# A two-layer hybrid decoder trunk on one core: the second block's sliding attention weights are turned by VectorE and DRAM, and the delta values' trip by DRAM follows the small inverses

## The chip, the cores and the metric

The kernel runs on one core of one Trainium2 chip. The metric is device time in microseconds (us) of one execution. A core has TensorE for matmuls (PE in the profile, with its weight loads as PEld), VectorE (DVE), ScalarE (ACT), GpSimd (POOL) and SyncE (SP), each with its own queue of instructions; DMAs are issued here by SP and POOL. Transfers of weights are issued by SP, those by DRAM that this text speaks of by POOL.

## The reference

Two decoder layers on 256 tokens of width 1024. Each is a SwiGLU half step, then three token mixers on the same stream (a gated delta rule, a sliding-window attention with sinks, a cross attention to 256 memory rows), a gated merge with an output projection, and another SwiGLU half step, each of the three with a residual and a layer norm. The change touches the sliding attention and the delta rule's values:

```python
def sliding_window_attention(q, k, v, sinks):      # 8 heads in 2 groups of 4, dh 64, window 128
    nb = S_ // W                                   # 2 blocks of 128 queries
    ...
    s = jnp.einsum('bnqhgd,bnkhd->bnhgqk', qb, kb).astype(f32) * (dh ** -0.5)
    ...
    m = jnp.maximum(s.max(-1, keepdims=True), sink)
    p = jnp.exp(s - m)
    p = p / (p.sum(-1, keepdims=True) + jnp.exp(sink - m))
    o = jnp.einsum('bnhgqk,bnkhd->bnqhgd', p.astype(v.dtype), vb)

def gated_delta_rule(q, k, v, g, beta):            # 4 heads, dk = dv = 128, chunks of 64
    ...
    sol = lax.linalg.triangular_solve(t_mat, rhs, left_side=True, lower=True, unit_diagonal=True)
```

A query block sees its own 128 keys and, for the second block, the 128 before them. So the weights p of the first block have one key block and those of the second have two.

## The kernel before, in words

All 256 tokens stay on the chip. Weights come as a stream of units of 128 x 1024 numbers: SP loads a unit into `raw`, ACT casts it to `whi` and DVE computes the remainder `wlo` (`unit`, line 104; `split`, line 124). Each product is three matmuls (`mm3`, line 139), high by high, high by low, low by high. The pool of `whi` has five buffers and that of `wlo` too (lines 42 and 43), so a unit's cast takes the buffer of the unit five before it and waits until PE has done that unit's matmuls.

`mixers` (line 560) holds the token mixers. Its matmuls are pinned: `keep_in_program_order` puts PE's work in the order in which the code is written. `weave` (line 145) runs a generator of matmul groups and calls small steps behind the group of a given number. ACT, DVE and POOL are ordered by a scheduler when the program is built; `issue_after` adds that an instruction stands behind another on the same engine's queue, and `held` does so for the last recorded instruction of each engine in the dictionary `late`. Within an engine the queue is fixed once the program is built.

The steps around the change, with block `tb` 0 or 1 (the first or second 128 tokens) and `hh` 0 or 1 (the first or second four of the eight heads):

- `w_scores(tb, hh)` (line 803): scores of the sliding attention on PE, mask, maximum, exponential and division on DVE and ACT; the weights stand as queries by keys in `wpr[tb, hh]`. Its reciprocal on DVE is `wpr["end"]`.
- `w_turn(tb, hh)` (line 832): turns them to keys by queries. Four PE transposes a key block (the line is 137, a helper's) into a PSUM bank `at`, then one copy a bank into `wpT[tb]` (line 840, ACT for key block 0, DVE for key block 1). For block 1 that is eight transposes and two copies for each `hh`.
- `w_values(tb)` (line 842): values times weights, two matmuls a key block, into one bank `at`, then a split into `oS` (buffers u6 and u7) by ACT and DVE.
- `inverses` (line 857): 16x16 triangular inverses on POOL in 15 steps, until line 883 writes `Y32`.
- `doubling(c)` (line 913): grows these to 32, 64 and 128, for both token blocks `c`, in steps of matmuls on PE into a bank `sm` and copies of it on ACT or DVE (buffers w0 to w3). `double` (line 970) runs one step of both. Each step's matmuls read what the step before copied.
- `begin_inverse` (line 974): one DVE transpose of `Y32`, which waits for POOL.
- `leave_v`, `back_v`, `land_v` (lines 635 to 650): the delta rule's values go from channels by tokens (`vT`, buffer u8) to tokens by channels (`vin`, u2). DVE turns 32x32 squares into `z`, POOL stores `z` to a DRAM tile `tv` in four DMAs a block (64 KB each, runs of 512 bytes), and loads it back in one DMA a block (256 KB); DVE scales it.
- `gates(n)` (line 1042): sigmoid gates, two halves of four units, twelve matmuls a unit, eight steps. `branch(n, o)` (line 1060): the branch's projection by four units, twelve matmuls a step, four steps; the first two steps read block 0 of `o`, the last two block 1.

The order is written at lines 1078 to 1108: `gates(0)`, `branch(0, oX)`, `gates(1)`, `branch(1, oS)`, `gates(2)`, `branch(2, oT)`. Before the change, `gates(1)` had `leave_v` behind step 3, `w_turn(1, 0)` and `back_v` behind step 5, `w_turn(1, 1)` behind step 6, and `w_values(1)` and `land_v` behind step 7.

## Time and profile before

| | us |
|---|---|
| timed runs, median of 3 | 1265.56 |
| timed runs, lowest to highest | 1264.87 to 1265.59 |
| the profiled execution's own time | 1265.74 |
| its span in the trace | 1263.8 |
| granted TensorE clock, mean | 0.998 |

| engine | busy us | share |
|---|---|---|
| PE | 1252.4 | 99% |
| DVE | 878.2 | 69% |
| ACT | 661.0 | 52% |
| POOL | 235.4 | 19% |

The span is what the trace holds; the execution's time is 1.9 us longer. A row of the timeline gives the start of an instruction (or of several alike, xN), how long it took, engine, line and operation, the tile written and the one read, shapes, and in brackets how long the engine was idle before it and what ended that. Matmuls are pipelined: each row's duration overlaps the next one's start, so the cost of a group on a busy PE is the difference of two starts. The changed steps lie in the two stretches from 325 to 385 us (layer 0) and from 950 to 1010 us (layer 1).

### The profile page before, as it was taken

The numbers are of one execution on the slowest core, as the hardware profiler recorded it, in microseconds if no ns is written. First come the engines' busy times: TensorE is split into PE (matmuls) and PEld (weight loads), VectorE is DVE, ScalarE is ACT, GpSimd is POOL, SyncE is SP. The second block draws the span as 40 slices with busy tenths as digits, with TensorE's granted clock in tenths as the row PEclk, the third lists the DMA queues.
The fourth block names the chain that finished last, engine by engine and source line by source line (L and its number), as shares of the span: only waits on it lengthen the run. The fifth ranks groups of instructions, "written<-read, shape, count | busy, mean of one in ns | idle before, by whom it ended". The sixth has DMA issues, their size and how long they took to land.

```text
span 1263.8 us, 18750 instructions
## 1 busy us (share of the span) xinstructions
PE 1252.4 (99%) x6884; PEld 1067.8 (84%) x6884; DVE 878.2 (69%) x1292; ACT 661.0 (52%) x982; POOL 235.4 (19%) x419
## 2 busy tenths in 40 slices
PE   9999999999999999999999999999999999999997
PEld 6888889999878888888888888899988788888886
DVE  6688567886668776665776665779777587666565
ACT  6456444655664544444354544365647654455441
POOL 1232102002331102221012220020033301122100
PEclk9999999999999999999999999999999999999999
DMA  8988867655554748877668876676564466577872
GB/s 283 317 271 280 262 217 216 224 180 133 170 152 150 242 140 258 243 241 221 221 205 240 260 261 204 213 237 214 163 157 140 130 200 217 184 242 246 243 224 77
DMA packets 80203, 267.76 MB, mean 212 GB/s; under 512 B 12912, under 2 KB 14352, under 8 KB 80112
## 3 DMA queue, kind: packets, MB, share of 16 engines
q1 hardware_dynamic: 66320, 232.40, 56.8%
q0 software_dynamic: 13648, 34.04, 10.5%
q8 instruction: 54, 0.88, 0.3%
q14 instruction: 37, 0.30, 0.1%
q10 hardware_dynamic: 144, 0.13, 0.0%
HBM read 249.58 MB, written 16.94 MB: 211 GB/s over the span
## 4 chain that ended last, share of the span: by engine, by line
PE 98%; DMA 1%; DVE 0%; SPq 0%; issue 0%; ACT 0%; DVEq 0%
PE acc L134 87%; PE at L134 4%; PE sm L134 3%; PE sm L137 1%; PE acc L332 1%; PE acc L333 1%; PE acc L335 1%; PE at L137 1%; DMA raw<-in_wst_dram 1%; DVE h L291 0%; DVE h L296 0%; SPq L115 0%; SPq L78 0%; ACT whi L125 0%; DVE bnst L277 0%
## 5 line engine op out<-in xcount | busy, mean ns | idle before, releaser
L125 DVE TENSOR_TENSOR wlo<-raw,whi 128x1024 fp32r<-128x1024 f32 (+2 forms) x405 | 487.0, 1210 | 258.3 <-ACT whi L125 256.4
L125 ACT CAST whi<-raw 128x1024 fp32r<-128x1024 f32 (+2 forms) x405 | 413.5, 1029 | 391.9 <-PE acc L134 305.3
L134 PE MATMUL acc<-whi,hT 128*128 128x512 f32 (+1 forms) x1824 | 562.9, 386 | 1.1 <-ACT whi L125 1.1
L134 PEld LDWEIGHTS acc<-whi,hT 128*128 128x128 f32 x1824 | 340.5, 188 | 71.6 <-ACT whi L125 2.9
L134 PE MATMUL acc<-wlo,hT 128*128 128x512 f32 (+1 forms) x912 | 350.7, 385 | 0.0
L134 PE MATMUL acc<-whi,u 128*128 128x512 f32 x812 | 259.7, 392 | 0.0
L134 PEld LDWEIGHTS acc<-wlo,hT 128*128 128x128 f32 x912 | 171.7, 188 | 32.8 <-DVE wlo L125 0.7
L134 PEld LDWEIGHTS acc<-whi,u 128*128 128x128 f32 x812 | 152.3, 188 | 32.0 <-DVE u L125 0.5
L134 PE MATMUL acc<-wlo,u 128*128 128x512 f32 x406 | 158.3, 390 | 0.0
L362 POOL DMA_DIRECT2D tr<-t x176 | 96.0, 552 | 315.3 <-DVE t L356 313.1
L134 PE MATMUL acc<-hT,whi 128*128 128x256 f32 x672 | 121.8, 284 | 0.0
L134 PEld LDWEIGHTS acc<-hT,whi 128*128 128x128 f32 x672 | 104.8, 192 | 0.0
L134 PE MATMUL acc<-hT,wlo 128*128 128x256 f32 x336 | 95.2, 283 | 0.0
L134 PEld LDWEIGHTS acc<-wlo,u 128*128 128x128 f32 x406 | 76.3, 188 | 15.4
L134 PEld LDWEIGHTS acc<-hT,wlo 128*128 128x128 f32 x336 | 64.4, 192 | 0.0
L363 POOL DMA_DIRECT2D pt<-tr x44 | 24.6, 558 | 192.1 <-DMA tr<-t 158.7
L353 ACT ACTIVATE t<-acc 128x256 f32<-128x256 f32 x88 | 33.4, 380 | 37.5 <-PE acc L134 37.4
L134 PE MATMUL acc<-u,u 128*128 128x512 f32 x186 | 46.4, 394 | 0.0
L354 DVE TENSOR_TENSOR t<-t,acc 128x256 f32<-128x256 f32 x88 | 36.7, 417 | 8.1 <-ACT t L353 3.9
L134 PEld LDWEIGHTS acc<-u,u 128*128 128x128 f32 x186 | 34.7, 188 | 7.5
L125 DVE TENSOR_TENSOR u<-pt,u 128x512 fp32r<-128x512 f32 x44 | 28.9, 657 | 10.0 <-ACT u L125 9.9
L589 DVE SCALAR_TENSOR_TENSOR t<-acc,cw,t 128x255 f32<-128x255 f32 (+2 forms) x72 | 34.5, 480 | 1.1
(250 smaller groups left out, 1177.1 us busy)
## 6 DMA issues: line engine op xcount, KB each, us to landing
raw<-in_wst_dram SPq DMA_DIRECT2D x409, 512.0 KB, 4.4
tr<-t POOLq DMA_DIRECT2D x176, 64.0 KB, 3.8
pt<-tr POOLq DMA_DIRECT2D x44, 256.0 KB, 5.3
raw<-in_wst_dram SPq DMA_DIRECT2D x16, 324.0 KB, 5.0
gB<-in_lnp_dram SPq DMA_DIRECT2D x6, 512.0 KB, 6.3
bB<-in_lnp_dram SPq DMA_DIRECT2D x6, 512.0 KB, 6.8
tn<-pp POOLq DMA_DIRECT2D x16, 128.0 KB, 3.8
pt<-tn POOLq DMA_DIRECT2D x8, 256.0 KB, 5.8
```

What stands on the lines that cost most here:

```text
L125: return nc.scalar.copy(hi, src).ins, nc.vector.tensor_tensor(lo, src, hi.bitcast(F32), op=ALU.subtract).ins
L134: return pe(nc.tensor.matmul(*a, **k))
L137: return pe(nc.tensor.transpose(*a))
L332: nc.tensor.matmul(ps, hT[0][:, k, ts], hi[:, c], start=k == 0, stop=False)
L333: nc.tensor.matmul(ps, hT[0][:, k, ts], lo[:, c], start=False, stop=False)
L335: nc.tensor.matmul(ps, hT[1][:, k, ts], hi[:, c], start=False, stop=k == KD - 1)
L353: act = nc.scalar.activation(t[:, :, tb, :], g, AF.Silu).ins
L354: ins = nc.vector.tensor_tensor(t[:, :, tb, :], t[:, :, tb, :], u, op=ALU.mult).ins
L362: nc.gpsimd.dma_start(d[:, :, q].rearrange("b c x -> c b x"), z[32 * q:32 * q + 32].rearrange("c (b x) -> c b x", b=4))
L363: back = nc.gpsimd.dma_start(y, d.rearrange("b c q x -> (b c) (q x)")).ins
L589: nc.vector.scalar_tensor_tensor(yc[:, j, d:], b[:, j, :S - d], w[:, t:t + 1], yc[:, j, d:], op0=ALU.mult, op1=ALU.add)
```

## The change

The second block's weights no longer pass PE. `w_turn` keeps the first block only. `w_leave(hh)` is new: two DVE transposes of 32x32 squares a half into `z` (buffers u8 and bB), four POOL stores of 128 KB into a DRAM tile `tw` (runs of 512 bytes), and two POOL loads of 256 KB, one a key block, into `wpT[1]`. The loaded tile has another order of its columns, so `w_values(1)` reads and writes with other access patterns, and its split is in two halves. `w_leave(0)` stands behind step 3 of `gates(1)`, `w_leave(1)` behind step 5, and `w_values(1)` moves from step 7 of `gates(1)` to step 1 of `branch(1, oS)`.

`leave_v` now holds the loads of `back_v` too, and moves from step 3 of `gates(1)` to step 3 of `branch(0, oX)`, ahead of `begin_inverse`: its DVE transposes stand behind `wpr["end"]` and ahead of `begin_inverse`'s, its stores behind `Y32`'s last instruction on POOL, its loads behind its stores.

The diff:

```diff
@@ -633,23 +633,25 @@
             return src[:, :, tb * P:(tb + 1) * P].rearrange("p h (q j) -> p q h j", q=4)
 
         def leave_v():
+            turned_v = []
             for tb in range(2):
                 z = T(p2, [P, 512], "t2", bufs=4)
-                nc.vector.transpose(z, squares(vT, tb))
+                with tc.issue_after(wpr["end"]):
+                    wpr["z"] = nc.vector.transpose(z, squares(vT, tb)).ins
                 d = T(pd, [4, 32, 4, P], "tv")
                 for a in range(4):
-                    nc.gpsimd.dma_start(d[:, :, a].rearrange("t j x -> j t x"), z[32 * a:32 * a + 32].rearrange("j (t x) -> j t x", t=4))
+                    with tc.issue_after(late["inverses"]):
+                        out_ = nc.gpsimd.dma_start(d[:, :, a].rearrange("t j x -> j t x"), z[32 * a:32 * a + 32].rearrange("j (t x) -> j t x", t=4)).ins
                 turned_v.append(d)
-
-        def back_v():
             for tb in range(2):
-                nc.gpsimd.dma_start(vin[:, tb].rearrange("p a h i -> p (a h i)"), turned_v[tb].rearrange("t j a x -> (t j) (a x)"))
+                with tc.issue_after(out_):
+                    late["pool"] = nc.gpsimd.dma_start(vin[:, tb].rearrange("p a h i -> p (a h i)"), turned_v[tb].rearrange("t j a x -> (t j) (a x)")).ins
 
         def land_v():
             for tb in range(2):
                 late["dve"] = nc.vector.tensor_tensor(vin[:, tb], vin[:, tb], kn[:, tb, :].unsqueeze(1).unsqueeze(3).to_broadcast([P, 4, 4, 32]), op=ALU.mult).ins
 
-        turned_v, sums_q = [], []
+        sums_q = []
 
         def leave_q():
             part = T(p2, [P, 4, 8], "oqs")
@@ -827,17 +829,29 @@
                 nc.scalar.activation(pr[:, h, :nk], pr[:, h, :nk], AF.Exp, bias=mxs[:, h // 2, h % 2:h % 2 + 1], accum_out=sums[:, h:h + 1])
             nc.vector.tensor_tensor(sums, sums, flat(sk), op=ALU.add)
             wpr["end"] = nc.vector.reciprocal(sums, sums).ins
-            [nc.scalar.mul(pr[:, h, :nk], pr[:, h, :nk], sums[:, h:h + 1]) for h in range(4)]
-
-        def w_turn(tb, hh):
+            late["act"] = [nc.scalar.mul(pr[:, h, :nk], pr[:, h, :nk], sums[:, h:h + 1]) for h in range(4)][-1].ins
+
+        def w_turn(hh):
             if hh == 0:
-                wpT[tb] = [T(p2, [P, 2, 4, P], "pt") for _ in range(tb + 1)]
-            for kb in range(tb + 1):
-                ps = at().rearrange("p (h k) -> p h k", h=4)
-                for h in range(4):
-                    transpose(ps[:, h, :], wpr[tb, hh][:, h, kb * P:(kb + 1) * P], ident)
-
-                (nc.vector.tensor_copy if kb else nc.scalar.copy)(wpT[tb][kb][:, :, 2 * hh:2 * hh + 2, :].rearrange("p v i q -> p i v q"), ps.rearrange("p (i v) q -> p i v q", v=2))
+                wpT[0] = T(p2, [P, 2, 4, P], "pt")
+            ps = at().rearrange("p (h k) -> p h k", h=4)
+            for h in range(4):
+                transpose(ps[:, h, :], wpr[0, hh][:, h, :P], ident)
+            nc.scalar.copy(wpT[0][:, :, 2 * hh:2 * hh + 2, :].rearrange("p v i q -> p i v q"), ps.rearrange("p (i v) q -> p i v q", v=2))
+
+        def w_leave(hh):
+
+            z = T(pu, [P, 1024], "bB" if hh else "u8")
+            for kb in range(2):
+                late["dve"] = nc.vector.transpose(z[:, kb * 512:(kb + 1) * 512], wpr[1, hh][:, :, kb * P:(kb + 1) * P].rearrange("p h (m x) -> p m h x", m=4)).ins
+            d = T(pd, [8, 32, 4, P], "tw")
+            for a in range(4):
+                out_ = nc.gpsimd.dma_start(d[:, :, a].rearrange("m x c -> x m c"), z[32 * a:32 * a + 32].rearrange("x (m c) -> x m c", m=8)).ins
+            if hh == 0:
+                wpT[1] = [T(p2, [P, 2, 512], "pt") for _ in range(2)]
+            for kb in range(2):
+                with tc.issue_after(out_):
+                    late["back"] = nc.gpsimd.dma_start(wpT[1][kb][:, hh], d[4 * kb:4 * kb + 4].rearrange("m x a c -> (m x) (a c)")).ins
 
         def w_values(tb):
             if not oS:
@@ -847,8 +861,16 @@
             for kb in range(tb + 1):
                 for kv in range(2):
                     hs = slice(kv * 64, kv * 64 + 64)
-                    matmul(pso[hs, :], swv[:, kb, hs], wpT[tb][kb][:, kv].rearrange("p h q -> p (h q)"), start=kb == 0, stop=kb == tb)
-            late["act"], late["dve"] = split(oS[0][:, :, ts], oS[1][:, :, ts], pso.rearrange("p (h k) -> p h k", h=4))
+                    if tb:
+                        o, w = pso[hs].rearrange("p (y i x) -> p y i x", y=8, i=2), wpT[1][kb].rearrange("p h (a i v x) -> p (h a) i v x", a=4, i=2, v=2)[:, :, :, kv]
+                    else:
+                        o, w = pso[hs], wpT[0][:, kv].rearrange("p h q -> p (h q)")
+                    matmul(o, swv[:, kb, hs], w, start=kb == 0, stop=kb == tb)
+            if tb:
+                for y in range(2):
+                    late["act"], late["dve"] = split(*(t[:, 2 * y:2 * y + 2, ts].rearrange("p i (a x) -> p i a x", a=4) for t in oS), pso[:, y * S:y * S + S].rearrange("p (a i x) -> p i a x", a=4, i=2))
+            else:
+                late["act"], late["dve"] = split(oS[0][:, :, ts], oS[1][:, :, ts], pso.rearrange("p (h k) -> p h k", h=4))
 
 
         qd = [slice(32 * i, 32 * i + 32) for i in range(4)]
@@ -880,8 +902,8 @@
                 n = 15 - j
                 nc.gpsimd.tensor_tensor(pr16[:, :, 0:n], ab[j // 8][:, j % 8, :, j + 1:16], y16[:, :, j:j + 1].to_broadcast([P, 8, n]), op=ALU.mult)
                 nc.gpsimd.tensor_tensor(y16[:, :, j + 1:16], y16[:, :, j + 1:16], pr16[:, :, 0:n], op=ALU.add)
-            nc.gpsimd.tensor_tensor(Y32.rearrange("p c h (d i) -> p (c h) d i", d=2), y16.unsqueeze(2).to_broadcast([P, 8, 2, 16]),
-                                    cs[:, C_BD:C_BD + 32].rearrange("p (d i) -> p d i", d=2).unsqueeze(1).to_broadcast([P, 8, 2, 16]), op=ALU.mult)
+            late["inverses"] = nc.gpsimd.tensor_tensor(Y32.rearrange("p c h (d i) -> p (c h) d i", d=2), y16.unsqueeze(2).to_broadcast([P, 8, 2, 16]),
+                                    cs[:, C_BD:C_BD + 32].rearrange("p (d i) -> p d i", d=2).unsqueeze(1).to_broadcast([P, 8, 2, 16]), op=ALU.mult).ins
             with tc.issue_after(post0.read):
                 nc.gpsimd.memset(Y, 0.0)
                 nc.gpsimd.memset(X64[qd[0], :, :, 32:64], 0.0)
@@ -973,7 +995,7 @@
 
         def begin_inverse():
 
-            with tc.issue_after(wpr["end"]):
+            with tc.issue_after(wpr["end"]), tc.issue_after(wpr["z"]):
                 nc.vector.transpose(W[:, 512:768], W[:, 768:1024])
 
 
@@ -1072,7 +1094,8 @@
                     dst = gt[tb] if n else mg[tb]
                     late["dve"] = nc.vector.scalar_tensor_tensor(dst[:, js], gt[tb][:, js], 1.0, ps, op0=ALU.add, op1=ALU.mult).ins
                     if n:
-                        nc.gpsimd.tensor_tensor(mg[tb][:, js], mg[tb][:, js], gt[tb][:, js], op=ALU.add)
+                        with tc.issue_after(late["back"]):
+                            nc.gpsimd.tensor_tensor(mg[tb][:, js], mg[tb][:, js], gt[tb][:, js], op=ALU.add)
                     yield
 
         weave(gates(0), {
@@ -1084,19 +1107,19 @@
             7: [lambda: w_scores(0, 0)],
             8: [lambda: w_scores(0, 1)]})
         weave(branch(0, oX), {
-            2: [lambda: w_turn(0, 0)],
-            3: [lambda: w_turn(0, 1), begin_inverse],
+            2: [lambda: w_turn(0)],
+            3: [lambda: w_turn(1), leave_v, begin_inverse],
             4: [lambda: w_scores(1, 0)]})
         weave(gates(1), {
             1: [double, lambda: w_values(0)],
             2: [lambda: w_scores(1, 1)],
-            3: [double, lambda: held(leave_v)],
-            5: [double, lambda: w_turn(1, 0), lambda: held(back_v)],
-            6: [double, lambda: w_turn(1, 1)],
-            7: [double, lambda: w_values(1), lambda: held(land_v)],
+            3: [double, lambda: held(lambda: w_leave(0))],
+            5: [double, lambda: held(lambda: w_leave(1))],
+            6: [double],
+            7: [double, lambda: held(land_v)],
             8: [double, lambda: held(leave_q)]})
         weave(branch(1, oS), {
-            1: [double],
+            1: [double, lambda: w_values(1)],
             2: [rec_v0],
             3: [rec_s1, lambda: held(land_q)],
             4: [rec_r1]})
```

Three places of the built program, all in layer 0. First **PE**, the second half of `gates(1)`: `sm` is a bank of a doubling step, `at` a bank of the turn, `acc` one of the gates, and the number after whi names the weight unit. Before:

```order
L134 MATMUL sm_3645<-w_468_2586,u_461_2577 32x32 x8
L134 MATMUL sm_3656<-w_468_2586,u_462_2578 32x32 x8
L137 MATMUL at_3669<-cs,pp_3394 128x128 x4
L137 MATMUL at_3675<-cs,pp_3394 128x128 x4
L134 MATMUL acc_3625<-whi_3684,hT_1602 128x512
...
L134 MATMUL acc_3626<-whi_3684,hT_1602 128x512
L134 MATMUL sm_3701<-w_468_2586,w_459_2575 32x32 x8
L134 MATMUL sm_3712<-w_468_2586,w_460_2576 32x32 x8
L137 MATMUL at_3723<-cs,pp_3506 128x128 x4
L137 MATMUL at_3729<-cs,pp_3506 128x128 x4
```

And after:

```order
L134 MATMUL sm_3659<-w_468_2586,u_461_2577 32x32 x8
L134 MATMUL sm_3670<-w_468_2586,u_462_2578 32x32 x8
L134 MATMUL acc_3639<-whi_3692,hT_1602 128x512
...
L134 MATMUL acc_3640<-whi_3692,hT_1602 128x512
L134 MATMUL sm_3709<-w_468_2586,w_459_2575 32x32 x8
L134 MATMUL sm_3720<-w_468_2586,w_460_2576 32x32 x8
L134 MATMUL acc_3639<-whi_3732,hT_1602 128x512
```

The four groups of transposes are gone; between the two doubling steps stand the twelve matmuls of one unit alone (whi_3684 before, the same unit is whi_3692 after).

Second **ACT**, from the gate's activation on to the cast for the next doubling step but one. L936 (before) and L958 (after) are the four copies of the first of these doubling steps, L943 and L965 those of the second, L840 the turn's copies, L658 and L660 the squares of `leave_q`. Before:

```order
L1057 ACTIVATE gt_3424<-acc_3426 128x512
L936 COPY w_459_2575<-sm_3645 32x4x32 x2
L936 COPY w_460_2576<-sm_3656 32x4x32 x2
L840 COPY pt_3667<-at_3669 128x2x2x128
L125 CAST whi_3849<-raw_3848 128x1024
L943 ACTIVATE w_469_2587<-sm_3701 32x4x32 x2
L943 ACTIVATE w_469_2587<-sm_3712 32x4x32 x2
L840 COPY pt_3667<-at_3723 128x2x2x128
L951 COPY w_468_2586<-w_468_2586 32x4x32 x3
L125 CAST whi_3855<-raw_3854 128x1024
```

And after:

```order
L1079 ACTIVATE gt_3440<-acc_3442 128x512
L125 CAST whi_3838<-raw_3837 128x1024
L958 COPY w_459_2575<-sm_3659 32x4x32 x2
L958 COPY w_460_2576<-sm_3670 32x4x32 x2
L973 COPY w_468_2586<-w_468_2586 32x4x32 x2
L965 ACTIVATE w_469_2587<-sm_3709 32x4x32 x2
L965 ACTIVATE w_469_2587<-sm_3720 32x4x32 x2
L973 COPY w_468_2586<-w_468_2586 32x4x32
L660 ACTIVATE t_665_3808<-u_388_2077 128x512
L660 ACTIVATE t_667_3813<-u_388_2077 128x512
L125 CAST whi_3844<-raw_3843 128x1024
```

The cast that stood behind the four copies (whi_3849) stands ahead of them (whi_3838, the same unit); the turn's copies are gone, and the squares come before the next cast. In order of allocation the units of this stretch are whi_3642, 3692, 3732 and 3776 (the second half of `gates(1)`) and 3826, 3832, 3838 and 3844 (`branch(1)`).

Third **POOL**, from the last step of `inverses` to the first addition of `branch(1)` (L1098); `tv` is the values' DRAM tile, `tw` the weights', L975 the eight copies of `Y32` into the diagonal of `Y`. After:

```order
L905 TENSOR_TENSOR w_468_2586<-t_531_3026,cs 128x256
L644 DMA tv_3381<-t_596_3379 32x4x128 x4
L644 DMA tv_3388<-t_598_3386 32x4x128 x4
L648 DMA u_392_2081<-tv_3381 128x512
L648 DMA u_392_2081<-tv_3388 128x512
L975 COPY w_469_2587<-w_468_2586 32x4x32 x8
L849 DMA tw_3610<-u_633_3607 32x8x128 x4
L854 DMA pt_3615<-tw_3610 128x512
L854 DMA pt_3616<-tw_3610 128x512
L849 DMA tw_3684<-bB_3681 32x8x128 x4
L854 DMA pt_3615<-tw_3684 128x512
L854 DMA pt_3616<-tw_3684 128x512
```

Before, the eight copies (then L953) came right behind the inverses, and the values' stores and loads (L641, L646) behind the copies, where the weights' stores and loads stand now. Layer 1 has the same orders.

## The prediction

> **What bounds the kernel now.** I read the busy shares first, then the chain of work that ended last, then the windows around the place of the change.
>
> ```profile
> PE 1252.4 (99%) x6884; PEld 1067.8 (84%) x6884; DVE 878.2 (69%) x1292; ACT 661.0 (52%) x982; POOL 235.4 (19%) x419
> ...
> PE 98%; DMA 1%; DVE 0%; SPq 0%; issue 0%; ACT 0%; DVEq 0%
> ...
> 340.00:375.00 35.00, 35.00 (x341) 26.66 (x336) 23.94 (x42) 25.91 (x62) 9.37 (x19) 1.00 0.59 176
> ```
>
> The first row gives each engine's busy time, the second the engines' shares of the chain, the third the busy time of PE, PEld, DVE, ACT and POOL in the 35 us of layer 0 that the change touches (then granted clock, DMA share, GB/s). PE is busy all 35 us at full clock. Its matmuls stand in program order, so work taken from PE there shortens the kernel one for one, and any wait of PE lengthens it one for one. DVE, ACT and POOL have room on average; what counts is what each has queued in front of the thing PE needs next.
>
> **The 16 transposes that PE loses.** The next rows are PE's timeline (start, duration, what), at the second block's two turns.
>
> ```profile
> 356.11 0.89 PE L134 MATMUL sm<-w,u 32*32 32x32 f32 x32
> 356.93 1.09 PE L137 MATMUL at<-cs,pp 128*128 128x128 f32 x8
> 357.78 0.47 PE L134 MATMUL acc<-whi,hT 128*128 128x512 f32 x1
> ...
> 360.38 0.39 PE L134 MATMUL acc<-whi,hT 128*128 128x512 f32 x1
> 360.70 0.89 PE L134 MATMUL sm<-w,w 32*32 32x32 f32 x32
> 361.52 1.09 PE L137 MATMUL at<-cs,pp 128*128 128x128 f32 x8
> 362.37 0.47 PE L134 MATMUL acc<-whi,hT 128*128 128x512 f32 x1
> ...
> 982.00 1.09 PE L137 MATMUL at<-cs,pp 128*128 128x128 f32 x8
> 986.59 1.09 PE L137 MATMUL at<-cs,pp 128*128 128x128 f32 x8
> ```
>
> Matmuls overlap, so starts are subtracted: eight transposes cost 357.78 - 356.93 = 0.85 us, and 362.37 - 361.52 = 0.85 us again. That is 1.70 us a layer; the last two rows are the same places in layer 1. Removed in all: **-3.40 us**. The page "VectorE: DVE Perf Modes" of the Trainium skill (sections The three transpose paths and Rules for kernel authors) speaks against this edit: it gives a 128x128 transpose to TensorE if PSUM will do as destination, since VectorE turns only 32x32 blocks, and puts one at 390 ns on TensorE. At 390 ns in a row the 32 transposes would be an estimated 12.5 us and the edit far larger; in this trace eight take 0.85 us, and the measurement decides.
>
> **What ACT then does to PE.** The doubling steps of the inverse (line 913 on) go PE, ACT copy, PE. The step at 356.11 writes a bank; ACT copies it (L936, four copies); the step at 360.70 reads the copies. Between the two, PE now runs eight transposes and twelve matmuls of a gate unit. ACT's rows of that stretch:
>
> ```profile
> 357.36 1.71 ACT L830 ACTIVATE pp<-pp,sums 128x256 f32<-128x256 f32 x4
> 358.97 0.58 ACT L1057 ACTIVATE gt<-acc 128x512 f32<-128x512 f32 x1
> 359.56 1.08 ACT L936 COPY w<-sm 32x128 f32<-32x128 f32 x4
> ...
> 361.15 1.05 ACT L125 CAST whi<-raw 128x1024 fp32r<-128x1024 f32 x1
> 362.09 1.11 ACT L943 ACTIVATE w<-sm 32x128 f32<-32x128 f32 x4
> ...
> 365.40 1.04 ACT L125 CAST whi<-raw 128x1024 fp32r<-128x1024 f32 x1 [0.64 <-PE acc L134]
> ```
>
> Before, the copies end at 359.56 + 1.08 = 360.64, just as PE arrives: no loss. In ACT's new order, shown with the change, the cast whi_3838 stands **ahead of these copies**. The pool of whi has five buffers (line 42); in order of allocation the units are 3692, 3732, 3776, 3826, 3832, 3838, so whi_3838 takes the buffer of whi_3692, and that is the unit of the twelve matmuls between the two doubling steps. So ACT waits for PE's last matmul of that unit, casts, and copies only then, while PE, with nothing else next in its order, waits for the copies. ACT runs its queue in order; nothing lets the copies pass the cast.
>
> The price, in layer 0. PE's twelve matmuls begin at 356.93 instead of 357.78, so the last starts at 360.38 - 0.85 = 359.53 and ends 0.39 later, 359.92. How soon a cast follows is seen at the other such place:
>
> ```profile
> 364.97 0.39 PE L134 MATMUL acc<-whi,hT 128*128 128x512 f32 x1
> ```
>
> It ends at 365.36 and the cast of the fence above starts at 365.40: 0.04 us. So the cast starts at 359.96; the next ACT instruction starts 0.94 later (361.15 to 362.09), at 360.90; four copies take 1.08, until 361.98. The doubling step has two halves (one for each 128-token block), 0.41 us each (361.52 - 360.70 = 0.82 for both), and the second needs all four copies: it starts at 362.02 and ends at 362.43. Free of the wait, PE would start its next unit at 362.37 - 1.70 = 360.67. The wait is thus 362.43 - 360.67 = **1.76 us a layer, 3.52 us in two**. It is given by the static order and row durations; with the cast or a copy 0.3 us quicker or slower I bound it by 1.3 and 2.3 us a layer.
>
> The next doubling step needs nothing that is late: its copies (1.11 us from about 362.5) end 1.7 us before PE has done another unit.
>
> **The values' matmuls, moved.** w_values(1) leaves the seventh step of gates(1) for the first step of branch(1):
>
> ```profile
> 365.91 1.94 PE L134 MATMUL at<-pt,swv 128*64 128x512 f32 x8
> 367.78 0.50 PE L134 MATMUL acc<-whi,hT 128*128 128x512 f32 x1
> ...
> 374.74 1.14 PE L134 MATMUL sm<-w,w 64*64 64x64 f32 x16
> 375.81 0.50 PE L134 MATMUL acc<-whi,u 128*128 128x512 f32 x1
> ```
>
> They cost 367.78 - 365.91 = 1.87 us at either place; their moving operand now comes in runs of 32 elements, as that of line 1012's matmuls does already, and I give that nothing. PE will come to them at 375.81 - 1.87 + 0.06 = 374.00, the 0.06 being 1.76 - 1.70. The evacuation, now in halves, is ACT, DVE, ACT, DVE; its full-size rows are these:
>
> ```profile
> 367.89 0.58 ACT L125 CAST u<-at 128x512 fp32r<-128x512 f32 x1 [1.00 <-PE at L134]
> 368.51 0.69 DVE L125 TENSOR_TENSOR u<-at,u 128x512 fp32r<-128x512 f32 x1 [0.81 <-ACT u L125]
> ```
>
> At most 2 x (0.58 + 0.69) = 2.5 us in series, with less for half sizes. The first reader of the second block's half comes after another twelve matmuls of branch(1), 360.70 - 357.78 = 2.92 us by the rows above, and line 1012's four besides. So the evacuation is covered; if ACT or DVE came to it 0.5 us late, PE would lose about 0.1 us.
>
> **The trips by DRAM.** DVE and POOL rows of layer 0, and POOL's of layer 1:
>
> ```profile
> 333.62 0.45 DVE L977 STREAM_TRANSPOSE w<-w 128x256 f32<-128x256 f32 x1 [3.65 <-POOL w L883]
> 353.39 1.26 DVE L638 STREAM_TRANSPOSE t<-u 128x512 f32<-128x512 f32 x2
> ...
> 350.36 2.28 POOL L953 COPY w<-w 32x128 f32<-32x128 f32 x4 [16.77 <-DVE w L927]
> 353.19 1.27 POOL L953 COPY w<-w 32x128 f32<-32x128 f32 x4 [0.54 <-DVE w L927]
> 354.41 4.45 POOL L641 DMA_DIRECT2D tv<-t  x8
> 360.57 0.56 POOL L646 DMA_DIRECT2D u<-tv  x1 [1.71 <-DMA tv<-t]
> 362.01 0.55 POOL L646 DMA_DIRECT2D u<-tv  x1 [0.88 <-DMA tv<-t]
> ...
> 979.48 4.44 POOL L641 DMA_DIRECT2D tv<-t  x8
> 986.33 0.56 POOL L646 DMA_DIRECT2D u<-tv  x1 [2.41 <-DMA tv<-t]
> ```
>
> The delta values' trip first. Its two DVE transposes (1.26 us) now lie in the 3.65 us in which DVE waits for POOL's inverses: nothing. Its eight stores, the wait and two loads (354.41 to 362.56, 8.2 us of POOL) move into the 16.77 us that POOL waits before the copies at 350.36: nothing, and they leave POOL free for the new trips. Behind them stand only those copies, with 8 us to spare.
>
> The weights' trip takes the vacated place on DVE: two transposes per half, the first pair at 353.39, done at 354.65, the second after ACT's scaling at 357.36 + 1.71 = 359.07, done at 360.4. DVE loses two copies (L840) and one pair of transposes, gains two pairs: 1.2 us more a layer, in idle time. On POOL, four stores of 128 KB and two loads of 256 KB per half. The nearest rows for issue and landing (the issue durations are minimum, median, maximum in ns; the page's rows end in KB and median us to landing):
>
> ```profile
> L410 POOL DMA_DIRECT2D tn<-pp x16: 550/550/557, 191.1 to 826.5; - x16
> L417 POOL DMA_DIRECT2D pt<-tn x8: 747/750/766, 199.6 to 832.2; - x8
> ...
> pt<-tn POOLq DMA_DIRECT2D x8, 256.0 KB, 5.8
> ...
> u<-tv POOLq DMA_DIRECT2D x4, 256.0 KB, 3.8
> ```
>
> I take 0.55 us an issue (L410 stores 128 KB too), and from the start of the fourth store to the start of the load behind it 4.4 us, the mean of what the tv stores show: 360.57 - (354.41 + 1.67) = 4.5, 362.01 - 358.3 = 3.7, 986.33 - (979.48 + 1.67) = 5.2. Then: stores from 354.70, fourth at 356.35; loads from 360.75, POOL free at 361.85; second half's stores from there, fourth at 363.5; loads at 367.9 and 368.45, landed 3.8 to 5.8 us later: 371.7 to 373.7 and 372.3 to 374.3. PE asks for the first at 374.00 and for the second 0.94 later (half of 1.87). **No wait**, with 0.3 us to spare or more. The ends: with 0.55, 3.7 and 3.0 it has landed at 370; with L417's 0.75 an issue, 5.2 a store and 5.8 a load, the first load lands at 376.9 and PE waits 2.9 us a layer. I take the middle, nearest to the tv rows of this same place. The page "DMA: Bandwidth & Descriptors" of the Trainium skill (section on the two cost components) prices a transfer at about 2.0 us plus bytes over 436 GB/s; by it a store is an estimated 2.3 us and a load 2.6, and the data would lie there well before PE asks; the tv rows, at 3.7 to 5.2, do not agree with so little, and the sum goes by the rows.
>
> **The sum.** Against the profiled execution (span 1263.8, its own time 1265.74): -3.40 + 3.52 + 0 = +0.12, so **1265.9 us**. The median of the three timed runs is 1265.56; the 0.18 between is inside their spread of 0.72, and I leave the sum as it stands.
>
> **Rivals.** A measurement of this kernel can tell about 0.2% (2.5 us) from no change.
>
> 1. *ACT's order costs nothing.* Then the transposes' full 3.40 us show: 1262.3. For it: PE is 98% of the chain. Against: the order is fixed when the program is built, and the cast's buffer is released only by the matmuls that PE does just before it needs the copies. Only a wait under 0.45 us a layer gives over 0.2%. Chance 0.09.
> 2. *The trip lands late (slower).* Place: the first matmul of w_values(1), PE standing. It decides once the second half's loads land after 374.0; at 1.2 us of wait a layer the loss passes 0.2%, and at the late end of 2.9 us it is 5.8 us: 1268.3 to 1271.7. For it: layer 1's 5.2 us, the second half's stores queue behind the first half's loads on POOL, and stores of 512-byte runs are twice as many as tv's. Against: the middle of every row. Chance 0.15.
> 3. *The change doesn't do what it says*: w_values(1) finds its operand but the removed matmuls leave PE's other starts where they were. PE's order shows the transposes gone, so only the wait above can keep the starts in place, and that is the forecast itself.
>
> **How the numbers follow.** The forecast, a gain and a wait that cancel, 0.76: with the wait's bounds of 1.3 and 2.3 us a layer, 1264.9 to 1266.9; with up to 1.1 us of late landing a layer, up to 1268.1. The range leaves out rival 1's full gain and the larger part of rival 2: 1263.0 to 1268.2. Faster by over 0.2%: 0.09, nearly all rival 1; slower by over 0.2%: 0.15; within: 0.76.
>
> **What would show it.** Right: in PE's rows of each layer a gap of about 1.7 us ahead of the second 32x32 doubling step after the removed turns, released by ACT; on ACT a cast that waits for PE right ahead of the four copies; no PE wait for DMA at w_values(1); the group L137 at<-cs,pp down from 80 to 48. Wrong: PE without a gap there (rival 1), or a PE wait put down to the loads of pt (rival 2). The forecast falls with either, and with a slower w_values(1) than 1.87 us.

## The result, and the profile after

| | before | after |
|---|---|---|
| median of the comparison, us | 1265.53 (8 runs, 1264.79 to 1266.68) | 1270.04 (8 runs, 1267.91 to 1272.99) |
| the profiled execution's own time, us | 1265.74 | 1270.28 |
| its span, us | 1263.8 | 1268.5 |
| granted TensorE clock, mean | 0.998 | 0.995 |

The ratio is 1.0035, with an interval of 1.0024 to 1.0046: the changed kernel is slower by 4.5 us. The forecast was 1265.9 with a range up to 1268.2. From the profile's page, the busy time of the engines and the engines' shares of the chain of waits:

```profile
PE 1252.8 (99%) x6852; PEld 1067.2 (84%) x6852; DVE 881.1 (69%) x1298; ACT 658.8 (52%) x980; POOL 249.1 (20%) x443
...
PE 90%; DVE 3%; DMA 2%; issue 2%; POOL 2%; ACT 0%; SPq 0%; DVEq 0%; POOLq 0%
```

The group of PE's transposes, with its count, busy time and mean ns:

```profile
L137 PE MATMUL at<-cs,pp 128*128 128x128 f32 x48 | 6.5, 272 | 0.0
```

PE's share of the chain fell from 98% to 90%: it now waits. The group of transposes is down from 80 to 48, so 32 are gone, as the change says. The view of what PE waited for (us in total, times, longest):

```profile
PE sm L134 <- ACT w L958: 3.4, 2, 1.7
PE at L134 <- DMA pt<-tw: 1.5, 1, 1.5
```

Both waits of the prediction's list are there: two for ACT's copies, one in each layer, and one for the weights' trip. PE's timeline in layer 0, from the doubling step ahead of the first removed turn on (start, duration, what, and in brackets the idle time before and what ended it):

```profile
355.40 0.89 PE L134 MATMUL sm<-w,u 32*32 32x32 f32 x32
...
358.85 0.39 PE L134 MATMUL acc<-whi,hT 128*128 128x512 f32 x1
360.92 1.14 PE L134 MATMUL sm<-w,w 32*32 32x32 f32 x32 [1.68 <-ACT w L958]
...
362.48 0.63 PE L134 MATMUL acc<-wlo,hT 128*128 128x512 f32 x1
362.90 1.05 PE L134 MATMUL acc<-whi,hT 128*128 128x512 f32 x2
...
366.52 0.69 PE L134 MATMUL sm<-w,w 32*32 32x32 f32 x16
...
376.79 1.94 PE L134 MATMUL at<-pt,swv 128*64 128x512 f32 x8 [1.54 <-DMA pt<-tw]
...
381.52 1.05 PE L134 MATMUL sm<-u,w 128*128 128x128 f32 x8
```

The same places of layer 1:

```profile
983.74 0.89 PE L134 MATMUL sm<-w,u 32*32 32x32 f32 x32
...
989.26 1.21 PE L134 MATMUL sm<-w,w 32*32 32x32 f32 x32 [1.68 <-ACT w L958]
...
994.82 0.69 PE L134 MATMUL sm<-w,w 32*32 32x32 f32 x16
...
1008.22 1.05 PE L134 MATMUL sm<-u,w 128*128 128x128 f32 x8
```

And ACT's rows between the two doubling steps of layer 0 (from the timeline of all engines):

```profile
359.27 1.04 ACT L125 CAST whi<-raw 128x1024 fp32r<-128x1024 f32 x1 [0.43 <-PE acc L134]
...
360.34 1.07 ACT L958 COPY w<-sm 32x128 f32<-32x128 f32 x4
```

The forecast wait is where it was put: PE ends its unit at 358.85 + 0.39 = 359.24, the cast starts at 359.27, the copies only behind it at 360.34, and PE stands until 360.92. But look at the rows after the wait. In the next unit the matmuls are 0.42 us apart (362.48 to 362.90); in the rows of before twelve of them took 2.92 us, 0.24 each. The windows of that stretch say why (the stretch, its length, busy time of PE, PEld, DVE, ACT and POOL with counts, then **granted clock**, DMA share, GB/s):

```profile
358.71:362.13 3.42, 1.74 (x36) 1.20 (x35) 3.35 (x5) 2.87 (x9) 0.80 (x2) 1.00 0.75 283
362.00:363.00 1.00, 1.00 (x5) 0.81 (x4) 0.18 (x1) 0.94 (x5) 1.00 (x2) 0.56 0.50 74
363.00:364.00 1.00, 1.00 (x4) 0.80 (x3) 0.00 (x0) 0.95 (x3) 1.00 (x3) 0.50 0.65 188
364.00:365.00 1.00, 1.00 (x3) 0.75 (x3) 0.82 (x2) 0.67 (x2) 0.77 (x2) 0.50 0.94 356
365.00:366.00 1.00, 1.00 (x5) 0.77 (x4) 1.00 (x3) 0.00 (x0) 0.00 (x0) 0.73 1.03 385
...
986.77:990.18 3.41, 1.73 (x35) 1.19 (x34) 3.33 (x5) 2.87 (x8) 0.28 (x1) 1.00 0.82 318
990.18:993.59 3.41, 3.41 (x17) 2.67 (x13) 1.41 (x3) 2.72 (x8) 3.16 (x6) 0.50 0.75 228
```

Between 362 and 366 us the clock was halved for 2 x 0.44 + 2 x 0.50 + 2 x 0.50 + 2 x 0.27 = 3.4 us in all (a window with a mean of 0.56 has 0.88 us at half clock in its 1 us, and so on). Windows of 0.05 us put its edges at 362.13 and 365.54; the first row is cut there, and the two rows of layer 1 are cut in the same way, from 990.18 to 993.59. This was not foreseen.

To sort the loss by cause, PE's rows are cut into two stretches that hold the same work in both kernels: A from the doubling step sm<-w,u to the one with 16 matmuls, B from there to the step sm<-u,w (the first of the delta rule's recurrence). Before, with the two turns in A:

```profile
356.11 0.89 PE L134 MATMUL sm<-w,u 32*32 32x32 f32 x32
...
365.29 0.69 PE L134 MATMUL sm<-w,w 32*32 32x32 f32 x16
...
378.67 1.05 PE L134 MATMUL sm<-u,w 128*128 128x128 f32 x8
```

A is 9.18 us, and 9.18 - 1.70 = 7.48 without the turns; B is 13.38. After, layer 0 has 366.52 - 355.40 = 11.12 and 381.52 - 366.52 = 15.00, layer 1 has 11.08 and 13.40. So A lost 3.6 us in each layer, and B 1.6 us in layer 0 alone. Together, with the turns' gain, 3.56 + 1.92 = 5.5 us. The two profiled executions differ by 4.5; most of the rest is at the start, since A begins at 355.40 instead of 356.11, and such starts differ between the runs of this study, from 354.57 to 356.15.

### The profile page after: what moved, and what is told of

It reads as the page before. It is cut to its first block, busy times and chain, and to the rows that moved or that the text cites. A ratio compares the mean times of both kernels' runs of the same rounds, so it can differ in the third digit from the quotient of the medians.

```text
span 1268.5 us, 18740 instructions
## 1 busy us (share of the span) xinstructions
PE 1252.8 (99%) x6852; PEld 1067.2 (84%) x6852; DVE 881.1 (69%) x1298; ACT 658.8 (52%) x980; POOL 249.1 (20%) x443
## 4 chain that ended last, share of the span: by engine, by line
PE 90%; DVE 3%; DMA 2%; issue 2%; POOL 2%; ACT 0%; SPq 0%; DVEq 0%; POOLq 0%
PE acc L134 81%; PE at L134 3%; PE sm L134 2%; DMA raw<-in_wst_dram 1%; PE sm L137 1%; PE acc L335 1%; PE acc L332 1%; PE acc L333 1%; DVE wlo L125 1%; DMA tw<-bB 0%; POOL t L904 0%; POOL t L903 0%; POOL l L894 0%; DMA tw<-u 0%; DVE h L291 0%
## 5 line engine op out<-in xcount | busy, mean ns | idle before, releaser
L1098 POOL TENSOR_TENSOR u<-u,gt 128x512 f32<-128x512 f32 x16 | 20.6, 1290 | 85.6 <-DVE gt L1095 85.6
```

The lines of the kernel that those rows point to most:

```text
L1098: nc.gpsimd.tensor_tensor(mg[tb][:, js], mg[tb][:, js], gt[tb][:, js], op=ALU.add)
```

## The experiments

Three questions: is the loss in A the copies' wait alone, and what makes the clock fall? Is the trip late by its queue or by the DMA engines? Does the moved trip of the delta values cost anything? Each kernel was timed beside the kernel before on the same chip; ratios are against it, with their intervals.

**1. The copies ahead of the cast.** Only ACT's order (and DVE's remainder with it) changes.

```diff
             for e, o in pairs:
-                nc.scalar.copy(M[o, :, e], ps[o])
+                wpr["M"] = nc.scalar.copy(M[o, :, e], ps[o]).ins
...
-            us = [unit() for _ in range(4)]
+            us = [unit(behind=wpr["M"] if n == 1 and i == 2 else None) for i in range(4)]
```

> The changed kernel, with ACT's cast of branch(1)'s third unit held behind the four copies that PE waits for; nothing else moves on PE or POOL. Theory A (the cast makes PE idle for 1.7 us a layer, and the idle time itself makes the granted clock fall to 0.50 for about 4 us): the wait of PE for the copies falls from 1.68 to about 0.4 us, the clock stays at 1.00 behind it, the matmuls of the next unit are 0.23 us apart instead of 0.43. PE then reaches the values' matmuls about 3.3 us earlier while the weights' trip lands as before, so in layer 0 the wait there grows from 1.5 to 4-5 us, and in layer 1 one of 0 to 3 us appears: 1266.5 to 1270.0 us. Rival B (the slow matmuls come from the traffic of the weights' trip at that time): the clock rows behind the step stay at 0.5, and the doubling step waits 0.4: 1268 to 1270 us.

1270.94 us (1270.11 to 1271.64), ratio 1.0041 (1.0029 to 1.0054). What PE waited for:

```profile
PE at L134 <- DMA pt<-tw: 5.1, 2, 3.0
...
PE sm L134 <- ACT w L958: 0.4, 2, 0.2
```

The windows of the wait for the trip in layer 0 and behind it, cut at the edges of the halved stretch:

```profile
371.46:374.87 3.41, 0.44 (x8) 0.30 (x6) 0.10 (x1) 0.75 (x2) 2.88 (x4) 1.00 0.68 227
374.87:378.28 3.41, 3.35 (x8) 0.77 (x8) 0.00 (x0) 0.00 (x0) 2.21 (x4) 0.50 0.05 4
```

The long wait for the copies is gone (1.68 to 0.2 us), and so is the slow stretch behind it: A is 8.06 us in layer 0. But PE now stands 3.0 us in layer 0 and 2.0 in layer 1 for the trip (4 to 5 and 0 to 3 were expected), and behind them the clock is 0.50 again, for 3.41 us in layer 0, as long as in the changed kernel. So the fall follows whatever wait PE has, one for a DMA as well as one for ACT, and it is not bound to the doubling step. The time was a little above the expected range, which did not count this.

**2. No trip.** Stores and loads of tw are left out; the second block's values read a block-turned tile.

```diff
-            d = T(pd, [8, 32, 4, P], "tw")
-            for a in range(4):
-                out_ = nc.gpsimd.dma_start(d[:, :, a].rearrange("m x c -> x m c"), ...).ins
             if hh == 0:
-                wpT[1] = [T(p2, [P, 2, 512], "pt") for _ in range(2)]
-            for kb in range(2):
-                with tc.issue_after(out_):
-                    late["back"] = nc.gpsimd.dma_start(wpT[1][kb][:, hh], ...).ins
+                wpT[1] = [z[:, kb * 512:(kb + 1) * 512].unsqueeze(1).to_broadcast([P, 2, 512]) for kb in range(2)]
...
```

> The changed kernel without the weights' trip through DRAM: w_values(1) reads the block-turned tile of the first half directly, so its output is not the reference's; stores and loads of tw are left out, the orders of PE, ACT and DVE stay. Theory A: the 1.7 us wait for the copies and the half clock for 4 us behind it stay in both layers, only the wait for the trip in layer 0 (1.5 us) goes: 1268.5 us. Rival B (the trip's traffic slows the matmuls): clock 1.00 behind the wait, 1264.8 us.

1267.26 us (1265.07 to 1268.45), ratio 1.0009 (1.0000 to 1.0018): between the two theories. The profiled execution (1265.80 us) shows why. PE's timeline:

```profile
355.32 0.89 PE L134 MATMUL sm<-w,u 32*32 32x32 f32 x32
...
360.84 1.14 PE L134 MATMUL sm<-w,w 32*32 32x32 f32 x32 [1.68 <-ACT w L958]
...
364.87 0.69 PE L134 MATMUL sm<-w,w 32*32 32x32 f32 x16
...
378.26 1.05 PE L134 MATMUL sm<-u,w 128*128 128x128 f32 x8
```

Its windows of the wait and behind it (where they are cut is explained below the table of runs 2 to 5):

```profile
357.57:360.98 3.41, 1.73 (x12) 1.11 (x11) 2.94 (x5) 2.92 (x7) 0.00 (x0) 1.00 0.58 197
360.98:364.40 3.42, 3.42 (x43) 2.87 (x42) 1.41 (x3) 3.27 (x11) 0.00 (x0) 1.00 0.53 150
```

The same wait of 1.68 us, and this time the clock stays at 1.00. A is 9.55, B 13.39. Of the 11 executions timed, four have a mean clock of 0.998 and take 1265.07 to 1266.20 us; seven have 0.996 or 0.997 and take 1266.88 to 1268.45. So with one and the same program the fall comes in some executions and not in others. It comes although no trip is left, so rival B, the trip's traffic, falls. Without the fall the wait costs 9.55 - 7.48 = 2.07 us a layer, and the fall in the changed kernel 11.12 - 9.55 = 1.57 and 11.08 - 9.55 = 1.53 more.

**3. Both edits.** Edits 1 and 2 together.

> Both edits: the copies ahead of the cast, and no trip through DRAM (the stores and loads of tw are left out, the values are computed from block-turned weights). Theory A: neither wait nor half clock is left, and the 16 transposes a layer are gone: 1265.5 - 3.4 + 2 x 0.3 (a rest of the wait for the copies) = 1262.7 us. Rival C (the half clock comes from the 32x32 matmuls or from the missing transposes, not from PE standing idle): the clock still falls to 0.5, 1266.5 us.

1262.89 us (1261.84 to 1263.48), ratio 0.9976 (0.9966 to 0.9985), mean clock 0.998 or 0.999 in all ten runs. Theory A gave 1262.7. The 32x32 matmuls and the missing transposes lower no clock by themselves: rival C falls.

**4 and 5. Idle time by itself.** From the kernel of run 3, PE's wait is made longer by needless copies on ACT ahead of the four (one in the first run, four in the second).

```diff
+            for _ in range(4 * (c == 0)):
+                wpr["slow"] = nc.scalar.copy(bank[:, P:512], cs[:, 0:384]).ins
             for e, o in pairs:
-                wpr["M"] = nc.scalar.copy(M[o, :, e], ps[o]).ins
+                with tc.issue_after(wpr["slow"]):
+                    wpr["M"] = nc.scalar.copy(M[o, :, e], ps[o]).ins
```

> The kernel without the trip (stores and loads of tw left out) and with the copies first, and one needless ACT copy (128x384) put ahead of the four copies, so that PE idles about 0.8 us there in each layer instead of 0.2. By idle time alone: 1262.9 + 2 x 0.6 = 1264.1 us. If a wait of this length also lowers the clock now and then, as one of 1.7 us seems to, the times spread up to 1268 us and the mean clock of those runs falls from 0.998 to 0.996 or 0.997; I expect none or few.

> As the run before, with four needless ACT copies (and three of line 973's copies between them by the scheduler's choice): PE idles about 3.2 us in each layer. By idle time alone: 1262.9 + 2 x 3.0 = 1268.9 us at clock 0.998. If the clock falls for about 4 us whenever PE idles long enough (cost 1.9 us each): 1272.7 us, with 0.995 in every run. If it still happens by chance: a spread from 1269 to 1273 us.

One copy: 1263.23 us (1262.25 to 1264.73), mean clock 0.998 or 0.999 in all 11 runs. Four: 1271.45 us (1270.48 to 1273.72), 0.994 to 0.996 in all five. What PE waited for in the latter:

```profile
PE sm L134 <- ACT w L962: 6.2, 2, 3.1
```

Its windows of the wait and behind it, in layer 0 and then in layer 1:

```profile
358.05:361.46 3.41, 0.37 (x2) 0.00 (x0) 2.01 (x4) 3.25 (x11) 0.00 (x0) 1.00 0.52 154
361.46:364.88 3.42, 3.37 (x37) 2.92 (x38) 1.58 (x2) 3.30 (x9) 0.00 (x0) 0.50 0.02 5
364.88:368.29 3.41, 3.41 (x9) 2.18 (x9) 2.11 (x4) 0.13 (x1) 0.54 (x1) 0.50 0.54 154
...
986.10:989.52 3.42, 1.49 (x7) 0.91 (x5) 2.75 (x5) 3.30 (x10) 0.00 (x0) 1.00 0.53 172
989.52:992.93 3.41, 2.24 (x38) 1.98 (x39) 1.02 (x1) 3.28 (x10) 0.00 (x0) 1.00 0.02 5
```

Both layers have a wait of 3.1 us; in layer 0 the clock is down for 6.83 us behind it, in layer 1 not at all. So a longer wait makes the fall likelier, not certain.

| PE's wait in a layer, us | run | executions | of these with a mean clock below 0.998 | median, us |
|---|---|---|---|---|
| 0.2 | 3 | 10 | 0 | 1262.89 |
| 0.75 | 4 | 11 | 0 | 1263.23 |
| 1.68 | 2 | 11 | 7 | 1267.26 |
| 3.1 | 5 | 5 | 5 | 1271.45 |

Of the 72 executions of the kernel before that were timed beside runs 1 to 12, two have a mean clock below 0.998.

What decides is where the wait lies. The halved stretches begin at 362.13 and 990.18 in the changed kernel, and at 374.87 and 1002.93 in run 1. Both pairs are 628.05 us apart, although the waits ahead of them end 628.34 us apart in the one and 627.34 in the other; in run 1's layer 0 the clock falls 0.06 us before the wait ends. 628.05 is 184 times 3.413. Each of these four stretches lasts 3.41 us, and that of run 5 twice as much. When PE has no more work at the end of a span, the clock is halved too, and in the changed kernel that begins at 1263.25, 264.00 times 3.413 behind 362.13. So the granted clock changes on a beat of 3.413 us that does not follow PE's waits.

The rows with uneven edges above are beats; those of run 2 are counted back from the halved stretch at the end of its span, 1258.69 - 264 x 3.4133 = 357.57. In the changed kernel both waits fall into one beat whole (3.42 - 1.74 = 1.68 and 3.41 - 1.73 = 1.68 us idle), and the next beat is at half clock. In layer 1 of run 5 an edge cuts the wait of 3.1 us into 1.93 and 1.17, and nothing falls. In all 14 profiles every whole beat at full clock in which PE was idle for 2.0 us or more was followed by half clock, and none with under 1.6 us was. In between lie the two of the changed kernel, with a fall, and two without: run 5's 1.93 us and run 2's 1.68 in layer 0. In the two with a fall most of PE's other time went to the 32x32 matmuls of the doubling step, in the two without to 128x128 ones; that the small ones count for less is a guess that no run tested.

The needless copy of run 4 cost 0.3 us rather than the 1.2 expected: in run 3 the second half of the doubling step waits once more for its copies (its row is 1.14 us long, run 4's 0.89), which the needless copy only puts together into one wait.

**6 and 7. The wait filled.** If PE standing idle lowers the clock, needless work on PE in that place must keep it up. The first try put 24 transposes into a bank of the doubling steps.

> The run with four needless ACT copies (PE waits 3.1 us in each layer; 1271.45 us, clock 0.994 to 0.996), with 24 needless 128x128 transposes on PE in that wait, about 24 x 0.106 = 2.5 us, into an unused part of a PSUM bank; the trip through DRAM is left out as there. The results that PE waits for come at about the same time. If it is PE standing idle that lowers the clock: no fall, clock 0.998 in all runs, 1268.0 to 1269.5 us. If it is the late copies, ACT's load or the stretch of the program: 0.995 again, 1271 to 1272 us.

1283.92 us (1283.14 to 1284.67), mean clock 0.993. It tells nothing on what was asked: that bank was itself still being read by the copies, so the transposes waited too, and ACT's order moved as well (the second softmax came ahead of the copies). PE's wait, by what it waited for:

```profile
PE sm L137 <- ACT w L963: 13.0, 2, 6.5
```

The second try uses a bank of the scores' pool.

```diff
+            if c == 0:
+                spare = at()
+                for _ in range(48):
+                    transpose(spare[:, 0:P], wpr[0, 0][:, 0, :P], ident)
             ps = part()
             for e, o in pairs:
                 for h in range(4):
                     matmul(ps[e, h], M[o, h, e], Y32[o, c, h], start=True, stop=True)
```

> The kernel without the trip (left out as before), with one needless ACT copy and the second softmax of the weights ahead of the four copies on ACT, so that they end some 4 to 5 us after PE has finished its unit, and 48 needless transposes on PE in that place, into a PSUM bank of the scores' pool that is free by then: 48 x 0.106 = 5.1 us of work. PE has hardly anything left to wait for. If PE standing idle is what lowers the clock: 1.00 throughout, 0.998 in all runs, and per layer 5.1 us more than where nothing waits, that is 4.5 more than the kernel with copies first and no trip: 1262.9 + 2 x 4.5 = 1271.9 us. If late copies or ACT's load in this stretch lower it: 0.995 and 1275 us or more.

1271.55 us (1271.29 to 1271.95), mean clock 0.998 or 0.999 in all five. The timeline of layer 0:

```profile
358.63 5.40 PE L137 MATMUL at<-cs,pp 128*128 128x128 f32 x48
...
362.62 0.85 ACT L963 COPY w<-sm 32x128 f32<-32x128 f32 x4
```

The windows of the same place:

```profile
359.00:362.00 3.00, 3.00 (x30) 3.00 (x28) 0.34 (x2) 2.50 (x9) 0.00 (x0) 1.00 0.40 147
362.00:365.00 3.00, 3.00 (x52) 2.79 (x51) 2.75 (x5) 2.94 (x8) 0.00 (x0) 1.00 0.00 0
```

The copies end at 362.62 + 0.85 = 363.47, 4.8 us after PE has begun the needless work at 358.63; without that work this would be a longer wait than any above but run 6's. PE works through, the windows have the clock at 1.00, and no execution's mean falls. It is PE standing idle that lowers it, not the late copies and not ACT's load.

**8, 9 and 10. Getting the trip out of the way.** Edit 1, and on POOL the stores of both halves ahead of the loads (8); with that, the values one gate group later (9); edit 1 and the values later, the trip's order as in the changed kernel (10).

```diff
+            turned_w.append(d)
-            for kb in range(2):
-                with tc.issue_after(out_):
-                    late["back"] = nc.gpsimd.dma_start(wpT[1][kb][:, hh], ...).ins
+            for g, d in enumerate(turned_w if hh else ()):
+                for kb in range(2):
+                    with tc.issue_after(out_):
+                        late["back"] = nc.gpsimd.dma_start(wpT[1][kb][:, g], ...).ins
...
-            1: [double, lambda: w_values(1)],
-            2: [rec_v0],
+            1: [double],
+            2: [lambda: w_values(1), rec_v0],
```

> The copies ahead of the cast, and on POOL the four stores of the second half issued ahead of the two loads of the first half (in the changed kernel they stand behind them and so wait until the first half has landed in DRAM). Theory A and a trip that is late by its queue: stores of the second half from 359.8 instead of 362.4 us, the loads landed by 371 to 374 us against PE's asking at about 372: a wait of 0 to 2 us a layer is left, 1263 to 1266.5 us, below the kernel before at the lower end. Rival D (the trip is late because the DMA engines are full with weight loads, whatever the order on POOL): the wait stays near 4 us a layer, 1267 to 1270 us.

> The copies ahead of the cast, the stores of both halves ahead of the loads, and the values' matmuls of the second block one gate group (twelve matmuls, 2.8 us) later, ahead of the step rec_v0. Theory A (what is left over the kernel without the trip is PE's wait for the landing): PE asks at about 375 instead of 372 us in layer 0, the loads land by 373.4 and 375.4 us; the wait falls to 0 to 0.4 us, no clock drop follows, 1262.5 to 1263.8 us, below the kernel before. Rival E: the values' results reach the next gate group too late (ACT's and DVE's two copies each stand between), PE waits 0.5 to 1.5 us a layer there instead: 1264 to 1266 us.

> The changed kernel with two edits of order alone: the copies ahead of the cast, and the values' matmuls of the second block one gate group later, ahead of rec_v0; the stores and loads of the trip stay where the changed kernel has them. If the landing is at 374.9 us in layer 0 and 1002.3 in layer 1, as with the copies first alone, PE asks at 375.0 us and the wait is 0 to 0.5 us: 1263 to 1264 us. If the loads land later still when PE's pace changes, a wait of 1 to 2 us in one layer: 1264.5 to 1266 us.

| run | median, us | ratio | PE's wait for the trip, us |
|---|---|---|---|
| 8 | 1265.38 (1263.64 to 1267.67) | 0.9998 (0.9990 to 1.0007) | 1.15 and 0.94 in layer 0, none in layer 1 |
| 9 | 1263.06 (1262.17 to 1264.26) | 0.9978 (0.9969 to 0.9986) | none |
| 10 | 1262.47 (1262.06 to 1264.23) | 0.9973 (0.9961 to 0.9985) | none |

Run 8 leaves a wait in layer 0, of 2.1 us against the 4 us a layer of rival D, and five of its 11 executions have a mean clock of 0.996 or 0.997. Runs 9 and 10 have 0.998 or 0.999 in all. The order on POOL is not needed; a later asking is. How late the trip is, and where, the changed kernel's own POOL rows tell. Layer 0:

```profile
354.25 2.34 POOL L849 DMA_DIRECT2D tw<-u  x4 [0.49 <-DVE u L846]
361.33 1.12 POOL L854 DMA_DIRECT2D pt<-tw  x2 [4.74 <-ACT w L958]
362.44 2.34 POOL L849 DMA_DIRECT2D tw<-bB  x4
372.75 1.12 POOL L854 DMA_DIRECT2D pt<-tw  x2 [7.98 <-issue]
```

Layer 1:

```profile
982.58 2.34 POOL L849 DMA_DIRECT2D tw<-u  x4 [0.49 <-DVE u L846]
989.90 1.11 POOL L854 DMA_DIRECT2D pt<-tw  x2 [4.97 <-PE sm L134]
991.00 2.34 POOL L849 DMA_DIRECT2D tw<-bB  x4
997.90 1.11 POOL L854 DMA_DIRECT2D pt<-tw  x2 [4.56 <-DMA tw<-bB]
```

From the fourth store's start (362.44 + 3 x 0.585 = 364.20) to the load behind it pass 8.6 us for the second half of layer 0; for the other three it is 5.3, 5.6 and 5.1. Of the four rows of loads only the last names a store as what ended the wait. The view of the tile `tw` has its DMAs land 2.4 to 7.1 us after their issue, so 8.6 us need not be landing alone; the rest is not sorted. In the changed kernel's windows above, the DMA engines are busy to 0.94 and more from 364 to 366, at 356 and 385 GB/s, when these stores are under way. In run 8, where these stores are issued from 360.03 instead of 362.44, their loads follow at 369.07 instead of 372.75, still 7.3 us behind the fourth store: the queue on POOL is a part of the delay and not all of it. That the weight loads are the rest is argued from these rows; no run took the loads away.

**11. The copies ahead of the tanh too.** Run 9, with a priority for the four copies.

```diff
             for e, o in pairs:
-                wpr["M"] = nc.scalar.copy(M[o, :, e], ps[o]).ins
+                with tc.high_priority(offset=40):
+                    wpr["M"] = nc.scalar.copy(M[o, :, e], ps[o]).ins
```

> The best kernel so far (copies ahead of the cast, stores of both halves ahead of the loads, values later; 1263.06 us), with the four copies ahead of the gate's tanh on ACT as well. What is left of PE's wait for them (0.62 us a layer: 8.06 us from the doubling step to the one after next, against 7.48 where nothing waits) should go: 1263.06 - 1.2 = 1261.9 us. Rival: the tanh, now behind the cast, is late for the bank that it frees, or the next copies are, and the gain is given back: 1263 us.

1262.22 us (1261.28 to 1262.29), ratio 0.9965 (0.9952 to 0.9977), the fastest of the study. PE waits for neither copies nor trip; A is 7.60 us:

```profile
355.20 0.89 PE L134 MATMUL sm<-w,u 32*32 32x32 f32 x32
...
362.80 0.69 PE L134 MATMUL sm<-w,w 32*32 32x32 f32 x16
```

It lies 0.84 us below run 9, of 1.2 expected, and its runs overlap with those of runs 9 and 10.

**12. The delta values' trip alone.** The kernel before, with only that part of the change.

```diff
-            3: [lambda: w_turn(0, 1), begin_inverse],
+            3: [lambda: w_turn(0, 1), leave_v, begin_inverse],
...
-            3: [double, lambda: held(leave_v)],
-            5: [double, lambda: w_turn(1, 0), lambda: held(back_v)],
+            3: [double],
+            5: [double, lambda: w_turn(1, 0)],
```

> The kernel before with only the delta values' trip by DRAM moved right behind the small inverses, the weights turned by PE as before. Theory: this part costs and gains nothing, its transposes lie in DVE's idle time and its DMAs in POOL's wait, and ACT keeps the four copies ahead of the cast: 1265.6 us, within 0.7. Rival: the moved part disturbs ACT's order or the copies of line 975 and accounts for a part of the loss: 1267 to 1270 us.

1265.79 us (1265.05 to 1267.35), ratio 0.9999 (0.9990 to 1.0008). It costs and gains nothing.

## Why the prediction was wrong

| term, us | forecast | measured in the profiles |
|---|---|---|
| 32 transposes | -3.40 | -3.40 by before's rows; run 11, without waits, has A 1.58 shorter than before |
| PE's wait for ACT's copies | 2 x 1.76 | 2 x 2.07 (run 2) |
| lower clock behind that wait | not in the sum | 1.57 and 1.53 (both layers in this execution) |
| PE's wait for the weights' trip | 0 | 15.00 - 13.38 = 1.62 in layer 0, 0 in layer 1 |
| delta values' trip, moved | 0 | 0 (run 12) |
| sum | +0.12 | +5.5 (the two profiled executions differ by 4.5) |

*The transposes and the static order: right.* The cast of the unit that takes the buffer of the unit before the wait is where the order put it, it starts 0.03 us after PE's last matmul, and the four copies follow. Putting them first (run 1) takes that wait away.

*The price of the wait: the step that failed.* The prediction wrote "The wait is thus 362.43 - 360.67 = 1.76 us a layer" and carried only that into the sum: PE's idle time, and full speed behind it. The runs showed two things in its place. The wait itself is 2.07, because the copies begin 1.07 behind the cast instead of 0.94 and the second half of the doubling step ends later by the rest. And behind an idle time of 1.7 us the clock falls to 0.50 in part of the executions, which costs 1.5 us and more each time. Runs 4, 5 and 7 show that idle time is the cause; whether an execution has the fall goes, as far as the profiles tell, with where the wait lies on the beat of 3.413 us. The page "TensorE: Matmul & The Clock Gate" of the Trainium skill (Part 1, on the HAM clock gate) has the clock fall after at least one idle window of about 3.4 us, and says that this window runs freely and is not tied to the program. By the first sentence a wait of 1.7 us should cost nothing more than itself; the seven executions of 11 do not agree. With the second the traces agree: the halved stretches last 3.41 or 6.83 us and begin on one beat, 628.05 us apart, whatever PE's waits.

*"No wait" at the values' matmuls: mis-sized.* The issue took 0.585 us instead of 0.55, and from the fourth store to the load it took 5.3 and 8.6 us in layer 0, not 4.4. (The mean of the three tv figures is 4.5; that changes nothing.) The rows of the tv stores reached only to 5.2. It was the second rival, with its place and its mechanism named, and it came true in one layer of two. Run 1 shows that it and the copies' wait hide one another: without the copies' wait and the slow stretch behind it PE comes about 3 us earlier, and it stands 3.0 us for the trip in layer 0 instead of 1.5, and 2.0 in layer 1 instead of none.

*The first rival* (ACT's order costs nothing: 1262.3) is what is reached once the order is mended and the values are asked for later: 1262.22 to 1263.06 in runs 9 to 11. *The spread* of the changed kernel, 5.1 us against 1.9 of before, is a sign of its own: its mean clock is between 0.995 and 0.997 from run to run.

## What to carry to other kernels

On a TensorE that is busy all the time, a wait has two prices: the idle time and, from 1.7 us within one beat on in this kernel, possibly 3.4 us or more at half clock behind it, by where the beat lies in that execution. Needless work in the place of the wait kept the clock up (run 7), and moving the waiting step later cost nothing (runs 9 and 10). When work is taken from such an engine, look in the static order of the engine that feeds it for a wait on that same work, since what was cover for the one was also the release of the other. For a trip through memory, plan with the latest landing that any row shows, and ask for the data one group of work later than the middle says.

## What the runs showed of the hardware

- The granted TensorE clock fell to 0.50 behind idle times of 1.68 us (both layers of the changed kernel's profile; seven of 11 executions of run 2 by their mean clock), not once behind 0.75 us (11 executions of run 4), and not always behind 3.1 us (run 5's profile: 0.50 in layer 0, 1.00 in layer 1).
- It falls and rises on a beat of 3.413 us that does not follow the waits (628.05 us, 184 beats, between the falls of the two layers in the changed kernel and in run 1). It stayed down for one beat in these and for two in run 5. With 48 transposes of 128x128 in the place of the wait it stayed at 1.00 (run 7).
- The same 128 KB stores of 512-byte runs, from the same queue, took 5.1 to 8.6 us from their last issue to the load that waits for them.
- The strided moving operand of the second block's values, in runs of 32 elements, cost nothing: its eight matmuls take 1.94 us in the rows of before and after.
